# Four edits to the order of work in a two-layer attention and retention trunk: value products, column parts, sine tables, side work

## The chip, the cores and the metric

The kernel runs on one core of one Trainium2 chip. The metric is the device time of one execution in microseconds (us). The kernel before took 2097.04 us, the median of three runs (2094.75, 2097.04 and 2097.13 us).

The core's engines are named as the profile names them: PE (TensorE, the matrix products; PEld is its weight load), DVE (VectorE), ACT (ScalarE), POOL (GpSimd) and SP (SyncE, whose instruction queue starts the DMA transfers).

## What is computed

The input x is 2048 tokens by 1024 channels, in float32. Two layers do x <- x + W_out(concat(A * silu(gA), B * silu(gB))) on h = RMSNorm(x), and a last RMSNorm follows. The reference, cut to the core of one layer:

```python
hn = rms_norm(x, norm_gain)
aq, ak, av, ag, rq, rk, rv, rg = split(hn @ w_in)      # 8 sections of 512 columns
ya = chunked_rel_attention(aq, ak, av, rel_bias)       # 8 heads of 64, band of 9 chunks of 64
yr = chunkwise_retention(rq, rk, rv, cos, sin)         # 4 heads of 128, rotary phases
y  = concatenate([ya * silu(ag), yr * silu(rg)])
x  = x + y @ w_out
```

In the retention, q and k are turned by `cos` and `sin` of position times a frequency, a decayed product inside a chunk is added to a running state, and each head is normalised by its own RMS.

## The kernel before

**Tiles and products.** 2048 tokens are 16 tiles of 128, and four of them make a block n (0 to 3). A float32 matrix product is made of three float16 products of scaled halves (high by high, high by low, low by high), so that a product over 1024 channels is 24 matmuls: 8 channel tiles times 3.

**Stages.** The work of a layer l goes by four head groups s (each two attention heads and one retention head) and, within a group, by the four blocks n. That makes 32 stages (l, s, n). A stage has two halves of dense products:

- `dense_T` (L608 to L735) makes four transposed sections j: q, k, rotary q and rotary k. Each is 24 matmuls of 128x512 (L731) into one bank of the pool `psD`, which has two banks. `evacuate` then copies the bank with ACT (L631, L645) and takes the low half with DVE (`q_rest` L634, `k_rest` L648) one round later; that frees the bank. Sections 2 and 3 go through the rotation (L670, L673, L676), with tables loaded at L616 and L617. The very first stage, (0,0,0), has a form of its own for sections 0 and 1: column parts of 128 tokens (L712), because its tokens come tile by tile.
- `dense_V` (L737 to L772) makes, for each of the four token tiles a, the values of both kinds and both gates: 24 matmuls of 128x512 (L752) into a `psD` bank. ACT copies the value and takes Tanh for the gate (L760, L761, L762, L763), and DVE takes the rests one round later (L766, L768, L770). L770 is the last reader, so that it frees the bank. The gate tile `gt` is from the pool `gp`, with five buffers.

**Rounds.** A half is cut into 12 rounds of 8 matmuls. `run` (L1152) does this for each round: the matmuls of the round; `tick`, which does what was put off by `later(k, fn)`; one step of the attention of the *previous* stage; and some steps of side work, by `pull`. The emission order is the order of PE, DVE, ACT and POOL, each of which works its list strictly in order. SP's order is chosen by a scheduler after the start.

**Attention** goes by 8 units (tile a, head hx), with three rounds each. In the first round of unit i, `flow(1)` takes the value products `pv` of unit i-2 off the list `pipe`, and then `qk` of unit i follows. `qk` has the score matmuls (S, L800 and L801, into the single bank of `psS`), the DVE pass that adds the bias and takes the maximum (`sc`, L804, and `mq`, L806), the exponential (ACT, L807), the split into float16 halves `pq` (ACT L809, POOL L810), and one round later the transposing DMA to `pT` (SP, L812). `sc`, `pq` and `pT` have two buffers each. `pv` multiplies `pT` by the values (L820 to L822: 15 small matmuls for a full band), and `out_` (L826 to L835) divides by the sum, multiplies by the gate and stores, one round later. In the second round the retention's decayed products may follow, in the third the rest of the retention (L860, L864, L868, L880, L908, L916, L920 to L929); the unit's `pv` is then put on `pipe`.

**Side work** is a list of generators with step counts: the norms of the next block's tokens in the first group (`norms_from_input`: L205, L210, L227, L231, and the transposing DMAs L236 and L237 that write the block's `hT`), the rotary tables of the next block (`tables`, L81 to L134, with the two Sin activations at L121 and L122, each block's table being a list of small DVE steps), the scaling and splitting of the next group's weights (waits at L323 are for their mean squares), and `wout_first`, which readies the first two token tiles of the layer's output projection (`y_squares` L958, `y_scale` L961, `rows_hi` L227, `rows_lo` L233, and `y_turn`, again L236 and L237). `wout_first`'s row buffers share their two slots with `sc`. Per round, `run` pulls the number of steps that is the steps left over the rounds left, rounded up:

```python
todo = sum(max(b[1], 0) for b in bg)
...
pull(min(-(-todo // max(left, 1)), todo))
left -= 1
```

After the last group of a layer comes the output projection `wout` (L1105), whose first rounds lie beside the last attention.

Of the kernel before, what the change touches and what calls it, by code (L numbers as in the profile page):

```python
# [10 lines left out]
F32 = mybir.dt.float32  # L11
# [16 lines left out]
def hybrid_trunk(ctx: ExitStack, tc: tile.TileContext, x, pos, gain, gcol, w_in, w_out, rel, fgain,  # L28
# [54 lines left out]
    def tables(n, wk):  # L83

        ang, k, r, k2 = wk
        pi = k2.bitcast(I32)
        for hf in range(2):
            o = n * 512 + hf * 256
            sp.dma_start(pi[hf * 64:(hf + 1) * 64, :], pos[None, o:o + 256].to_broadcast([64, 256]))
        yield  # L90

        def mulsub(dst, kk, c):
            dve.scalar_tensor_tensor(out=dst, in0=kk, scalar=-c, in1=dst, op0=ALU.mult, op1=ALU.add)

        def rnd(dst, src, mul):
            dve.tensor_scalar(dst, src, mul, MAGIC, op0=ALU.mult, op1=ALU.add)
            dve.tensor_scalar(dst, dst, -MAGIC, None, op0=ALU.add)

        dve.tensor_copy(ang, pi)
        dve.tensor_scalar(ang, ang, invf_sb[:, 0:1], None, op0=ALU.mult)  # L100
        yield
        rnd(k, ang, 1.0 / P1)
        yield
        for c in (PA, PB, PC):
            mulsub(ang, k, c)
            yield
        dve.tensor_scalar(k2, k, -(PD + PE_), None, op0=ALU.mult)
        dve.tensor_tensor(k2, k2, ang, op=ALU.add)
        yield
        rnd(k2, k2, 1.0 / TWO_PI)  # L110
        yield
        for kk, c in ((k2, QA), (k, PD), (k2, QB), (k, PE_), (k2, QC)):
            mulsub(ang, kk, c)
            yield
        dve.tensor_scalar(ang, ang, PI_CL, -PI_CL, op0=ALU.min, op1=ALU.max)
        dve.tensor_scalar(k, ang, HALF_PI, -TWO_PI, op0=ALU.is_gt, op1=ALU.mult)
        yield
        dve.tensor_tensor(k, k, ang, op=ALU.add)
        dve.tensor_scalar(k, k, HALF_PI, PI_CL, op0=ALU.add, op1=ALU.min)
        yield  # L120
        act.activation(r, ang, AF.Sin)  # L121
        act.activation(k2, k, AF.Sin)  # L122
        yield
        dve.tensor_scalar(ang, r, -1.0, None, op0=ALU.mult)
        yield
        for hf in range(2):
            sl = slice(hf * 64, hf * 64 + 64)
            cs = slice(hf * 256, hf * 256 + 256)
            sp.dma_start(tab_d[n][0, 0:64, cs], k2[sl, :])
            sp.dma_start(tab_d[n][0, 64:128, cs], k2[sl, :])  # L130
            sp.dma_start(tab_d[n][1, 0:64, cs], ang[sl, :])
            sp.dma_start(tab_d[n][1, 64:128, cs], r[sl, :])
        tab_done.add(n)
        yield  # L134

    TAB_STEPS = 19

    class St:
        pass
# [468 lines left out]
    def dense_T(l, s, n, g, st):  # L608
# [96 lines left out]
        if first:  # L705
# [9 lines left out]
            for j in range(2):  # L715
                evacuate(j, ps[j])
                yield
        for j in range(2 if first else 0, 4):
            if j == 2 and not first:
                tab_load()  # L720
            if first:
                ps = psR.tile([P, 512], F32, tag="small", name=f"dT{nm}_{j}")
            else:
                ps = psD.tile([P, 512], F32, tag="dense", name=f"dT{nm}_{j}")
            while g.tdone <= j:
                pull(1)
            m = 0
            terms = ((g.h, hh), (g.l, hh), (g.h, hl))
            order = [(kt, w) for w in terms for kt in range(KT)] if j == 0 else [(kt, w) for kt in range(KT) for w in terms]
            for kt, (w_, h_) in order:  # L730
                pe.matmul(ps, w_[:, j, kt, :], h_[:, kt, :], start=(m == 0), stop=(m == 23))  # L731
                m += 1
                if m in (8, 16) or (m == 24 and first):
                    yield
            evacuate(j, ps)  # L735
            yield
# [41 lines left out]
    def attention(l, s, n, g, st, prev, nxt):  # L778
        units = []
        for a in range(4):  # L780
            for hx in range(2):
                units.append((a, hx))
        ya = {}

        def qk(a, hx):

            u = St()
            u.a, u.hx = a, hx
            u.nm = f"{l}_{s}_{n}_{a}_{hx}"
            u.nb = nb = min(5, 4 * n + a + 1)  # L790
            u.w = w = nb * P
            u.kts = [(st if t // 4 == n else prev, t % 4) for t in range(4 * n + a + 1 - nb, 4 * n + a + 1)]
            S = psS.tile([P, 1024], F32, tag="S", name=f"S{u.nm}")
            cs = slice(a * P, (a + 1) * P)
            cuts = sorted({0, nb} | {j for j in range(nb) if u.kts[j] == (st, 0) or j == 4})
            for j0, j1 in zip(cuts, cuts[1:]):
                q_, a_ = u.kts[j0]
                k_ = q_.k[:, hx, a_ * P:(a_ + j1 - j0) * P]
                o = S[:, j0 * P:j1 * P]
                pe.matmul(o, st.q[:, hx, 0, cs], k_, start=True, stop=False)  # L800
                pe.matmul(o, st.q[:, hx, 1, cs], k_, start=False, stop=True)  # L801
            v = b2.tile([P, 640], F32, tag="sc", name=f"sc{u.nm}")[:, 0:w]
            m = b2.tile([P, 1], F32, tag="mq", name=f"mq{u.nm}")
            dve.tensor_tensor_reduce(out=v, in0=S[:, 0:w], in1=g.bias[hx][:, 640 - w:640], scale=1.0, scalar=-3.0e38,  # L804
                                     op0=ALU.add, op1=ALU.max, accum_out=m)
            dve.tensor_scalar(m, m, g.nc[:, 0:1], LN_PSC, op0=ALU.mult, op1=ALU.add)  # L806
            act.activation(v, v, AF.Exp, bias=m[:, 0:1], scale=g.c[:, 0:1])  # L807
            pq = b2.tile([P, 1280], F16, tag="pq", name=f"pq{u.nm}")
            act.activation(pq[:, 0:w], v, AF.Copy)  # L809
            pool.tensor_tensor(pq[:, w:2 * w], v, pq[:, 0:w], op=ALU.subtract)  # L810
            u.p = b2.tile([P, 10, P], F16, tag="pT", name=f"pT{u.nm}")[:, 0:2 * nb, :]
            later(1, lambda: sp.dma_start_transpose(out=u.p, in_=pq[:, 0:2 * w]))  # L812
            return u

        def pv(u):
            t = 4 * n + u.a
            o = psR.tile([P, 512], F32, tag="small", name=f"o{u.nm}")
            for b, (q_, a_) in enumerate(u.kts):
                v_ = q_.v[:, a_, u.hx, :]
                pe.matmul(o[:, 0:65], u.p[:, b, :], v_[:, 0:65], start=(b == 0), stop=False)  # L820
                pe.matmul(o[:, 0:64], u.p[:, b, :], v_[:, 65:129], start=False, stop=False)  # L821
                pe.matmul(o[:, 0:65], u.p[:, u.nb + b, :], v_[:, 0:65], start=False, stop=(b == u.nb - 1))  # L822

            def out_():
                rl = b2.tile([P, 1], F32, tag="rl", name=f"rl{u.nm}")
                dve.reciprocal(rl, o[:, 64:65])  # L826
                dve.tensor_tensor(rl, rl, g.ka, op=ALU.mult)
                if u.hx == 0:
                    ya[u.a] = b2.tile([P, P], F32, tag="ya", name=f"ya{u.nm}")
                y = ya[u.a]  # L830
                vs = slice(u.hx * 64, u.hx * 64 + 64)
                dve.scalar_tensor_tensor(out=y[:, vs], in0=o[:, 0:64], scalar=rl[:, 0:1], in1=st.g[u.a][:, vs],
                                         op0=ALU.mult, op1=ALU.mult)
                if u.hx == 1:
                    sp.dma_start(y_d[t][:, s * P:(s + 1) * P], y)  # L835

            later(1, out_)

        ret = retention(l, s, n, g, st)
        for i, (a, hx) in enumerate(units):  # L840
            flow(1)
            u = qk(a, hx)
            yield
            if hx == 1:
                if a < 3:
                    decayed(l, s, n, g, st, a + 1)
                elif nxt is not None:
                    decayed(*nxt, 0)
            yield
            if hx == 1:  # L850
                next(ret, None)
            elif a == 0 and (l, s, n) == (0, 0, 0):
                decayed(l, s, n, g, st, 0)
            pipe.append(lambda u=u: pv(u))
            yield
# [294 lines left out]
        return groups[l, s]  # L1150

    def run(gen, att, thirds):  # L1152
        left = thirds
        for _ in gen:
            tick()
            if att[0] is not None and next(att[0], att) is att:
                att[0] = None
            ring["att_done"] = att[0] is None
            todo = sum(max(b[1], 0) for b in bg)
            if todo == 0 and bg:  # L1160
                todo = 1
            if bg:
                pull(min(-(-todo // max(left, 1)), todo))
            left -= 1

    def norms_from_input(ts, spaces, tab):
# [349 lines left out]
```

## Time and profile before

| quantity | value |
| --- | --- |
| median of three runs | 2097.04 us (2094.75 to 2097.13) |
| the profiled execution, its own time | 2094.75 us |
| its span in the trace | 2092.8 us |
| mean granted PE clock | 0.991 |
| busy: PE, DVE, ACT, POOL | 2004.4, 1343.8, 1141.3, 432.9 us |

The span is what the trace covers of one execution; the execution's own time is 1.95 us longer. In a timeline row the columns are the start in us, the duration in us, engine, line, operation, tiles and shape; what stands in brackets is the idle time of the engine just before, and what ended it. Matmuls overlap one another, so the distance between two starts is what a matmul costs, not its duration. In the view of waits a row gives what the engine waited for, then the total in us, the number of waits and the longest. In the view of windows the columns are the stretch, its length, the busy time and count of PE, PEld, DVE, ACT and POOL, the granted clock, the DMA share and GB/s.

### The profile page before, as it was taken

How to read it: one execution, taken by the hardware profiler on the slowest of the kernel's cores; microseconds unless marked ns; L12 is line 12 of the kernel's file. 1: busy time of each engine (PE TensorE's matmuls, PEld its weight loads, DVE VectorE, ACT ScalarE, POOL GpSimd, SP SyncE). 2: the span in 40 equal slices, each digit the busy share in tenths (PEclk: the TensorE clock that was granted, in tenths of full speed). 3: DMA queues.
4: the chain of work that ended last, by engine and by line, in shares of the span. 5: the costliest groups of instructions: out<-in, count | busy, mean ns of one | idle time of the engine just before them, and what ended most of it. 6: DMA issues, size and time to landing. Idle time of an engine off the chain costs nothing.

```text
span 2092.8 us, 39599 instructions
## 1 busy us (share of the span) xinstructions
PE 2004.4 (96%) x14014; PEld 1049.4 (50%) x14014; DVE 1343.8 (64%) x4031; ACT 1141.3 (55%) x2522; POOL 432.9 (21%) x509
## 2 busy tenths in 40 slices
PE   6888999999999999998999999999999999998998
PEld 4344455555555555444444555555555555554443
DVE  7676666666656666576654666666666667656643
ACT  7455665556565654455444546554655565455432
POOL 1022222222122212121000222222222222222100
PEclk9999999999999999999999999999999999999999
DMA  8767674557476764599965556655655776558874
GB/s 247 171 127 162 136 166 114 115 112 159 110 169 133 161 166 99 113 211 260 219 185 113 120 102 142 130 121 106 155 123 118 178 156 162 117 100 183 212 199 123
DMA packets 645702, 313.65 MB, mean 150 GB/s; under 512 B 459232, under 2 KB 602080, under 8 KB 645504
## 3 DMA queue, kind: packets, MB, share of 16 engines
q1 hardware_dynamic: 645504, 311.12, 66.4%
q8 instruction: 110, 1.80, 0.4%
q14 instruction: 88, 0.72, 0.1%
HBM read 123.26 MB, written 41.98 MB: 79 GB/s over the span
## 4 chain that ended last, share of the span: by engine, by line
PE 55%; DMA 7%; DVE 5%; ACT 3%; issue 1%; SPq 1%; POOL 0%; POOLq 0%; DVEq 0%; ACTq 0%
PE dT L731 18%; PE dV L752 15%; PE dO L1105 12%; DMA pT<-pq 2%; PE r L860 2%; PE S L801 2%; PE S L800 2%; PE o L820 1%; PE o L821 1%; PE o L822 1%; DVE sc L804 1%; DMA swp<-rot 1%; DMA yhy<-rhy 1%; ACT sc L807 1%; ACT pq L809 1%
## 5 line engine op out<-in xcount | busy, mean ns | idle before, releaser
L810 POOL TENSOR_TENSOR pq<-sc,pq 128x640 f16<-128x640 f32 (+4 forms) x256 | 323.8, 1265 | 1175.9 <-issue 590.7
L807 ACT ACTIVATE sc<-sc,mq,cT 128x640 f32<-128x640 f32 (+4 forms) x256 | 218.5, 853 | 558.1 <-DVE mq L806 413.7
L752 PE MATMUL dV<-whV,hTh 128*128 128x512 f16 x1024 | 354.5, 382 | 13.0 <-DVE gt L770 12.8
L731 PE MATMUL dT<-hTh,whT 128*128 128x512 f16 x1008 | 349.4, 382 | 14.7 <-DMA hTh<-hTl 9.6
L752 PE MATMUL dV<-wlV,hTh 128*128 128x512 f16 x1024 | 354.1, 381 | 0.0
L752 PE MATMUL dV<-whV,hTl 128*128 128x512 f16 x1024 | 354.0, 381 | 0.0
L731 PE MATMUL dT<-hTl,whT 128*128 128x512 f16 x1008 | 346.6, 379 | 0.0
L731 PE MATMUL dT<-hTh,wlT 128*128 128x512 f16 x1008 | 346.6, 379 | 0.0
L752 PEld LDWEIGHTS <-hTh 128*128 128x128 f16 x2048 | 197.3, 98 | 227.7 <-DVE gt L770 16.4
L731 PEld LDWEIGHTS <-whT 128*128 128x128 f16 x2016 | 192.9, 98 | 221.6 <-issue 24.1
L804 DVE CUSTOM_DVE_ANT_0 sc<-S,bias 128x640 f32<-128x640 f32 (+4 forms) x256 | 188.4, 736 | 78.8 <-PE S L801 61.1
L1105 PE MATMUL dO<-whO,yly 128*128 128x512 f16 x512 | 194.1, 379 | 2.4 <-DMA yly<-rly 2.4
L1105 PE MATMUL dO<-whO,yhy 128*128 128x512 f16 x512 | 194.0, 379 | 1.2 <-DVE gt L770 0.6
L1105 PE MATMUL dO<-wlO,yhy 128*128 128x512 f16 x512 | 194.0, 379 | 0.0
L809 ACT ACTIVATE pq<-sc 128x640 f16<-128x640 f32 (+4 forms) x256 | 171.5, 670 | 10.9 <-DMA pT<-pq 3.0
L1105 PEld LDWEIGHTS <-yhy 128*128 128x128 f16 x1024 | 99.6, 98 | 115.1 <-issue 0.8
L752 PEld LDWEIGHTS <-hTl 128*128 128x128 f16 x1024 | 99.7, 98 | 105.0 <-issue 2.8
L800 PE MATMUL S<-k,q 128*128 128x128 f16 (+3 forms) x592 | 143.1, 268 | 7.9 <-DVE mq L804 7.9
L731 PEld LDWEIGHTS <-wlT 128*128 128x128 f16 x1008 | 97.2, 98 | 101.8 <-issue 1.1
L820 PE MATMUL o<-v,pT 128*128 128x65 f16 x1120 | 129.6, 193 | 10.2 <-DMA pT<-pq 9.7
L801 PE MATMUL S<-k,q 128*128 128x128 f16 (+3 forms) x592 | 130.5, 268 | 0.0
L820 PEld LDWEIGHTS <-pT 128*128 128x128 f16 x1120 | 105.3, 97 | 49.2 <-DMA pT<-pq 21.3
(350 smaller groups left out, 3352.7 us busy)
## 6 DMA issues: line engine op xcount, KB each, us to landing
q<-qq SPq DMA_DIRECT2D x128, 128.0 KB, 2.7
yyy<-y_d SPq DMA_DIRECT2D x32, 512.0 KB, 4.6
stT<-in_w_in_dram SPq DMA_DIRECT2D x27, 512.0 KB, 4.8
stV<-in_w_in_dram SPq DMA_DIRECT2D x26, 512.0 KB, 4.5
k<-kk SPq DMA_DIRECT2D x128, 64.0 KB, 2.0
swp<-rot SPq DMA_DIRECT2D x64, 128.0 KB, 2.5
tabc<-tab SPq DMA_DIRECT2D x32, 256.0 KB, 2.7
tabs<-tab SPq DMA_DIRECT2D x32, 256.0 KB, 2.9
```

What stands on the lines that cost most here:

```text
L731: pe.matmul(ps, w_[:, j, kt, :], h_[:, kt, :], start=(m == 0), stop=(m == 23))
L752: pe.matmul(ps, h_[:, kt, a * P:(a + 1) * P], w_[:, kt, :], start=(m == 0), stop=(m == 23))
L800: pe.matmul(o, st.q[:, hx, 0, cs], k_, start=True, stop=False)
L801: pe.matmul(o, st.q[:, hx, 1, cs], k_, start=False, stop=True)
L804: dve.tensor_tensor_reduce(out=v, in0=S[:, 0:w], in1=g.bias[hx][:, 640 - w:640], scale=1.0, scalar=-3.0e38, op0=ALU.add, op1=ALU.max, accu ...
L807: act.activation(v, v, AF.Exp, bias=m[:, 0:1], scale=g.c[:, 0:1])
L809: act.activation(pq[:, 0:w], v, AF.Copy)
L810: pool.tensor_tensor(pq[:, w:2 * w], v, pq[:, 0:w], op=ALU.subtract)
L820: pe.matmul(o[:, 0:65], u.p[:, b, :], v_[:, 0:65], start=(b == 0), stop=False)
L821: pe.matmul(o[:, 0:64], u.p[:, b, :], v_[:, 65:129], start=False, stop=False)
L860: pe.matmul(out_, w_, m_, start=(i == 0), stop=(i + 1 == len(pairs)))
L1105: pe.matmul(ps, h_[:, kt, :], w_[:, kt, :], start=(m == 0), stop=(m == 23))
```

## The change

Four edits are made together.

1. `tables` gets one more empty step ahead of the two Sin activations, for every block but 0, and its count of steps goes from 19 to 20.
2. `dense_T` does sections 0 and 1 of stages (0,0,1), (0,0,2) and (0,0,3) in eight column parts of 128 tokens: three parts of q, three of k, the last of q, the last of k. A part is 24 matmuls of 128x128; there are 32 of them to a round, and six rounds as before. Both sections are evacuated in the sixth round.
3. In the attention, `qk` of unit i comes ahead of the value products, and these come one round later, in the unit's second round, ahead of `decayed`.
4. `run` pulls side steps by a running sum of steps left over rounds left, from a debt of one half, instead of rounding up in every round.

```diff
@@ tables
         dve.tensor_scalar(k, k, HALF_PI, PI_CL, op0=ALU.add, op1=ALU.min)
         yield
+        if n:
+            yield
         act.activation(r, ang, AF.Sin)
         act.activation(k2, k, AF.Sin)
-    TAB_STEPS = 19
+    TAB_STEPS = 20
@@ dense_T
-        for j in range(2 if first else 0, 4):
+        parts = (l, s) == (0, 0) and n > 0
+        if parts:
+            ps, m = [None] * 2, 0
+            for (j, a) in ((0, 0), (0, 1), (0, 2), (1, 0), (1, 1), (1, 2), (0, 3), (1, 3)):
+                if a == 0:
+                    ps[j] = psD.tile([P, 512], F32, tag="dense", name=f"dT{nm}_{j}")
+                cs = slice(a * P, (a + 1) * P)
+                for i in range(24):
+                    w_, h_ = ((g.h, hh), (g.l, hh), (g.h, hl))[i // KT]
+                    pe.matmul(ps[j][:, cs], w_[:, j, i % KT, :], h_[:, i % KT, cs], start=(i == 0), stop=(i == 23))
+                    m += 1
+                    if m % 32 == 0 and m < 192:
+                        yield
+                if a == 3:
+                    evacuate(j, ps[j])
+            yield
+        for j in range(2 if first or parts else 0, 4):
@@ attention
         for i, (a, hx) in enumerate(units):
+            u = qk(a, hx)
+            yield
             flow(1)
-            u = qk(a, hx)
-            yield
             if hx == 1:
@@ run
-        left = thirds
+        left, debt = thirds, 0.5
...
             if bg:
-                pull(min(-(-todo // max(left, 1)), todo))
+                debt += todo / max(left, 1)
+                pull(min(int(debt + 0.01), todo))
+                debt -= int(debt + 0.01)
             left -= 1
```

More of the change, by code (lines that the diff above doesn't have):

```diff
@@ L840, in attention @@
         for i, (a, hx) in enumerate(units):
-            flow(1)
             u = qk(a, hx)
             yield
+            flow(1)
             if hx == 1:
```

## The prediction

> **What bounds the kernel now.** I read the busy line of the page first, then the view of PE's waits, then windows of the places where those waits are, then timelines there.
>
> ```profile
> PE 2004.4 (96%) x14014; PEld 1049.4 (50%) x14014; DVE 1343.8 (64%) x4031; ACT 1141.3 (55%) x2522; POOL 432.9 (21%) x509
> PE dV L752 <- DVE gt L770: 12.8, 6, 4.9
> PE o L820 <- DMA pT<-pq: 9.7, 11, 2.2
> PE dT L731 <- DMA hTh<-hTl: 9.6, 1, 9.6
> PE S L800 <- DVE mq L804: 7.9, 4, 3.3
> PE msT L323 <- DVE mbT L316: 3.3, 3, 1.9
> PE msV L323 <- DVE ya L832: 2.9, 2, 1.6
> PE dT L731 <- DMA hTh<-rhn: 2.8, 1, 2.8
> ```
>
> PE is busy for 2004.4 of the span's 2092.8 us, so only some 88 us of idle time can be taken away, and the change adds no speed to a matmul. These seven rows of waits hold 49 us. The windows say where they lie (PE's busy time is the second number):
>
> ```profile
> 104.00:141.00 37.00, 27.64 (x162) 13.03 (x161) 27.33 (x77) 22.82 (x53) 7.67 (x11) 0.95 0.68 130
> 166.00:205.00 39.00, 29.46 (x209) 15.60 (x207) 27.29 (x74) 23.23 (x49) 7.98 (x10) 0.91 0.81 177
> 340.00:620.00 280.00, 278.64 (x2060) 148.31 (x2059) 185.31 (x605) 163.22 (x384) 66.09 (x74) 1.00 0.60 127
> 860.00:900.00 40.00, 33.77 (x239) 17.40 (x238) 25.22 (x76) 22.94 (x48) 6.74 (x7) 0.91 0.76 156
> 1870.00:1910.00 40.00, 33.56 (x251) 17.87 (x250) 25.25 (x72) 23.04 (x47) 7.16 (x8) 0.96 0.67 143
> ```
>
> From 340 to 620 us PE idles for 1.4 us: the steady stages have nothing to give. The idle time is in the first head group (9.4 us in 104 to 141, 9.5 in 166 to 205) and at the last stage of each layer (6.2 and 6.4 us of 40). The granted clock is below 1 in just these windows; a timeline shows what that is.
>
> ```profile
> 129.54 0.61 PE L752 MATMUL dV<-whV,hTh 128*128 128x512 f16 x1 [4.88 <-DVE gt L770]
> 129.94 0.63 PE L752 MATMUL dV<-whV,hTl 128*128 128x512 f16 x1
> 130.37 0.63 PE L752 MATMUL dV<-wlV,hTh 128*128 128x512 f16 x1
> 132.93 0.20 PE L820 MATMUL o<-v,pT 128*128 128x65 f16 x1
> 133.20 0.38 PE L800 MATMUL S<-k,q 128*128 128x512 f16 x1
> 133.63 0.38 PE L752 MATMUL dV<-wlV,hTh 128*128 128x512 f16 x1
> 133.85 0.38 PE L752 MATMUL dV<-whV,hTh 128*128 128x512 f16 x1
> ```
>
> After 4.88 us of idleness the matmuls start 0.43 us apart, and from 133 on 0.215 us (0.22 by these rounded rows). So such a wait costs its idle time and then about 0.2 us for each of the next 8 matmuls, 1.7 us here. The busy time hides that second part.
>
> **Sine tables a round later, and even side steps (first group, n = 1 and 2).** The wait above is for a bank. Its tile's matmuls were long over, and ACT stood before the Sin work:
>
> ```profile
> 115.95 0.38 PE L752 MATMUL dV<-wlV,hTh 128*128 128x512 f16 x1
> 124.36 1.28 ACT L121 ACT_TABLE_LOAD   x1
> 126.28 0.26 ACT L760 ACTIVATE v<-dV 128x128 f16<-128x128 f32 x1
> 126.54 1.28 ACT L761 ACT_TABLE_LOAD   x1
> ```
>
> PE ended tile a=1 at 116.2. ACT came to it at 126.28, after norms and then 1.92 us of Sin with its table, and lost 1.28 more going back to Tanh: 3.2 us. In the changed order Sin comes after a=1's evacuation and ahead of a=2's, whose bank is wanted three rounds later. The wait of 4.88 falls by 3.2, and at 1.7 us PE would not slow: 3.2 + 1.7 = 4.9. I take **+5** for n=1 (gains are positive); bounds -2 (Sin is as much in the way of a=2, and the even spread leaves more norm steps in the second half of the stage) and +8 (most of the 9.4, plus slow matmuls). For n=2 the window has the same idle time, but the norms' chain is as full: **+2.5**, bounds 0 to +6.
>
> **Column parts (first group).** The start of (0,0,1) and of (0,0,3):
>
> ```profile
> 69.37 1.29 SPq L237 DMA_TRANSPOSE hTl<-hTl  x1
> 74.73 2.92 SPq L237 DMA_TRANSPOSE hTl<-hTl  x1
> 78.11 0.69 DVE L670 TENSOR_TENSOR raw<-raw,tabc 128x512 f32<-128x512 f32 x1 [7.20 <-DMA swp<-raw]
> 78.91 3.26 PE L731 MATMUL dT<-hTh,whT 128*128 128x512 f16 x8 [9.64 <-DMA hTh<-hTl]
> 81.10 0.41 DVE L770 SCALAR_TENSOR_TENSOR gt<-gt,dV 128x256 f32<-128x256 f32 x1
> 204.90 3.40 PE L731 MATMUL dT<-hTh,whT 128*128 128x512 f16 x8 [2.81 <-DMA hTh<-rhn]
> ```
>
> PE waits 9.64 us for the last token tile's transposed copy, issued at 74.73; the three tiles before were issued by 70.7 (69.37 + 1.29). With parts, three q parts can run from about 73. But the three k parts need the second bank, and that is freed by L770 at 81.10, which stands in DVE's order behind the wait that ends at 78.11; this order is unchanged. So five parts are left at 81.5: 5 x 24 x 56 ns (below) = 6.7, to 88.2, and some 2 us more for a slow start after the new idle time. In the kernel before, 8 matmuls are done at 82.1 and 40 x 0.215 = 8.6 lead to 90.7. The gain of about 0.5 goes into section 2: both banks are evacuated in one round, and it has to wait for ACT and DVE. I take **-1**, bounds -4 and +2. At (0,0,3) the bank is free, the three early parts hide the wait of 2.81, and the 8 matmuls in 3.24 us (to 208.14, with 1.72 at full rate) go faster: 2.8 + 1.5 = 4.3, of which I take **+3** (0 to +4.3). The wait for the banks at section 2 costs (0,0,2) and (0,0,3) about 1 us each, an ACT copy and a DVE rest less 24 short matmuls: **-2** (-4 to 0).
>
> What the parts cost in themselves:
>
> ```profile
> 33.89 0.61 PE L712 MATMUL dT<-hTh,wlT 128*128 128x128 f16 x8
> 34.33 0.61 PE L712 MATMUL dT<-hTh,whT 128*128 128x128 f16 x8
> L820 PEld LDWEIGHTS <-pT x1120: 95/96/152, 93.4 to 1967.8; 128*128 128x128 f16 x187
> ```
>
> The first stage has such parts: eight in 0.44 to 0.45 us, 56 ns each. A section is 96 of them, 5.38 us, against 24 x 0.2155 = 5.17. Six sections: **-1.3**, bounds -26 (rival 4) and 0. The Trainium skill, "TensorE: Matmul & The Clock Gate", section "Back-to-back issue gap", gives about 81 ns a matmul for N=128 and 131 ns for N=512 in a stream of weight loads and matmuls; by it, estimated, a section would go from 3.1 to 7.8 us and the six would cost 28 us. The rows above, 56 and 215 ns, do not agree with it.
>
> **Even side steps elsewhere.** Group (0,0)'s last stage waits for mean squares (msT 3.3, msV 2.9 in all): fewer weight steps in its early rounds, **+2** (-2 to +5). The larger case is the last stage of each layer:
>
> ```profile
> 877.29 0.82 DVE L804 CUSTOM_DVE_ANT_0 sc<-S,bias 128x640 f32<-128x640 f32 x1 [5.11 <-DMA yhy<-rhy]
> 878.17 0.27 PE L800 MATMUL S<-k,q 128*128 128x128 f16 x1 [3.28 <-DVE mq L804]
> 879.19 0.63 PE L752 MATMUL dV<-wlV,hTh 128*128 128x512 f16 x1
> 883.87 0.38 PE L752 MATMUL dV<-whV,hTl 128*128 128x512 f16 x1
> 1891.00 0.27 PE L800 MATMUL S<-k,q 128*128 128x128 f16 x1 [3.18 <-DVE mq L804]
> ```
>
> The score buffer `sc` shares its slots with the row buffers of `wout_first`, so DVE's pass waits 5.11 us for the DMA that reads a row, and PE waits 3.28 for the score bank. Then 11 matmuls go 0.43 us apart (879.19 to 883.87), 2.3 us lost: 5.6 here, and the same at 1891.00 (3.18 and, the clock of that window being higher, some 1.4). Nineteen side steps are left for 12 rounds there: rounded up that is two a round, spread evenly 1.6. The second token tile's row then takes its slot only after this unit's `sc`. I take **+9.5** for both layers; bounds 0 (another unit meets the row instead) and +12.7 (the two windows' 12.6 us of idle time). What is late next is ACT's square of that tile, which nothing on PE needs at once.
>
> **Value products a round later.** The eleven waits for `pT` come to 9.7 us, the longest 2.2, the mean 0.9. A round has 8 x 0.2155 = 1.72 us of dense matmuls and the attention's besides, so one round covers all but the longest: **+8**, bounds 0 and +10. `qk` first means that PE no longer has the products ahead of S, nine in 0.27 us (132.93 to 133.20; fifteen, 0.45), while it waits for the score bank: **-1** over the run (-3 to 0). A wait is added on SP: `pT` has two buffers, so unit i+2's transposing DMA now waits for products of unit i in the same round, with the stores of L835 and L927 and other loads behind it in the queue. It costs nothing while `pq` is later still:
>
> ```profile
> L810 POOL TENSOR_TENSOR pq<-sc,pq 128x640 f16<-128x640 f32 (+4 forms) x256 | 323.8, 1265 | 1175.9 <-issue 590.7
> ```
>
> L804 (0.82) and L810 (1.27) alone are 2.1 us, over the 1.72 of a round, and the exponential and its copy come on top.
>
> **Sum.** 5 + 2.5 - 1 + 3 - 2 - 1.3 + 2 + 9.5 + 8 - 1 = 24.7 us. The profiled execution took 2094.75 us, with a span of 2092.8: it becomes 2070. The median is 2.3 higher, so the forecast is **2072**.
>
> **Rivals.**
>
> 1. *The first group gives nothing*: DVE, with 27.3 us in a window in which PE has 27.6, or a bank is late in the same way. The 7.5 us of its gains and losses go, or turn to -5: 24.7 - 7.5 - 5 = 12, 2080 to 2085. For it speaks the bank at 81.10.
> 2. *The `pT` waits move with the products*, as the DMAs come later by the added wait on SP: 2072 + 8 = 2080. Against it, the L810 row.
> 3. *Slower.* The fifth gate buffer: Tanh (L761) of tile a=3 needs the buffer that `out_` of unit 5 reads, and that is now emitted in the very round that ends a=3. If DVE is over a round (1.7 us) behind PE there, ACT stands, the bank comes late, and the next stage's second section waits. One us in each of 31 stages is 31: 2072 + 31 = 2103. It decides once ACT's delay is over the three rounds until that bank is wanted. ACT is usually early here, so I give it little:
>
> ```profile
> ACT v L760 <- PE dV L752: 22.4, 22, 3.4
> ```
>
> 4. *Weight loads bound the parts*: at the 96 ns of the LDWEIGHTS row a section takes 9.2 us, 4.05 more, 24 in all: 2072 + 23 = 2095. The skill's rule points here; the 56 ns speak against it.
> 5. *The score slot is met all the same* at the layer's end, by another unit: 2072 + 9.5 = 2081.
>
> **Numbers.** Forecast 0.56, rival 1 0.15, rival 2 0.09, rival 3 0.08, rival 4 0.04, rival 5 0.08. A measurement of this kernel tells about 0.2%, 4.2 us, from no change. Faster: 0.56 + 0.15 + 0.09 + 0.08, less a little for rivals that come together, 0.86; within 0.2%: rival 4 and that little, 0.06; slower 0.08. The range takes in rivals 1, 2 and 5 and two of them together (2092), and below it the upper bounds of the large terms: n=1 +3, layer ends +3, `pT` +2, n=2 +3.5, which give 2060. Rivals 3 and 4 are left out.
>
> **What would show it.** Right: the rows PE o <- pT and PE S <- mq nearly gone; no PE wait over 1 us in the last stage of either layer; the 4.88 row shrunk or gone; idle time at about 82 us, not before 73, in (0,0,1). Parts at 56 ns apart. Wrong: waits of ACT's L761 (then L779) for DVE in many stages, PE waits for L770 in the steady window, or side work that is late for the output projection (L1105 waiting for y's rows).

## The result, and the profile after

The changed kernel took 2124.95 us (median of four runs, 2122.47 to 2127.13), and the kernel before 2097.09 us beside it. The ratio is 1.0134, with a 95% interval of 1.0117 to 1.0152. It is 28 us slower where 25 us less were forecast, and outside the range given. The profiled execution has a span of 2124.8 us, against 2092.8 before.

In all that follows line numbers are those of the kernel at hand: from `dense_V` on the changed kernel's are 18 higher, so that L752, L770, L804, L832 and L860 before are L770, L788, L822, L850 and L878 after.

PE's busy line and waits in the changed kernel (columns of the waits: total in us, number, longest):

```profile
PE 2018.8 (95%) x14446; PEld 1075.7 (51%) x14446; DVE 1334.5 (63%) x4031; ACT 1142.9 (54%) x2522; POOL 431.1 (20%) x509
PE r L878 <- DVE ya L850: 19.7, 10, 2.7
PE dT L729 <- DVE gt L788: 12.8, 5, 6.3
PE S L818 <- DVE mq L822: 10.7, 8, 2.5
PE dV L770 <- DVE gt L788: 7.0, 4, 3.4
PE dT L749 <- DVE qq L636: 4.6, 3, 2.0
PE msT L325 <- DVE ya L850: 3.9, 9, 0.7
PE o L838 <- DMA pT<-pq: 2.3, 1, 2.3
```

Most of the waits at which the forecast aimed are down: `pT` from 9.7 us to 2.3, the dense bank in `dense_V` from 12.8 to 7.0, the transposed copies (9.6 and 2.8) gone. The score bank (`S`) is not: 10.7 us in 8 waits, against 7.9 in 4; the two long ones at the layer ends are down to one of 2.00 us (at 901.49), and others have come elsewhere (2.25 us at 112.55, 2.45 at 636.68, 2.24 at 1664.99). Three rows stand there that the kernel before did not have: retention products (`r`) and mean squares (`msT`) that wait for `out_` (tile `ya`), and the column parts (L729) that wait for the second dense bank.

The same windows as before, by time from the start:

```profile
104.00:141.00 37.00, 28.62 (x185) 14.16 (x184) 26.58 (x74) 19.96 (x44) 6.31 (x8) 0.91 0.49 103
166.00:205.00 39.00, 34.78 (x283) 19.22 (x281) 30.83 (x83) 23.55 (x51) 10.13 (x12) 1.00 0.75 152
340.00:620.00 280.00, 275.05 (x2015) 146.23 (x2013) 181.59 (x602) 157.42 (x370) 65.65 (x74) 1.00 0.57 121
860.00:900.00 40.00, 39.49 (x306) 21.43 (x305) 24.41 (x72) 20.49 (x42) 8.29 (x9) 1.00 0.64 120
1870.00:1910.00 40.00, 40.00 (x307) 21.63 (x306) 23.81 (x68) 17.42 (x39) 10.11 (x10) 1.00 0.54 101
```

From 340 to 620 us PE is now idle for 4.95 us where it was 1.4. Windows by time shift against each other (the last two now lie ahead of the waits at the layer ends), so the place of a loss is better read from the work. Each kernel has the same dense work, 7680 matmuls of 512 columns (a part of 128 columns counts a quarter). The table compares the start of the same one in two traces, in us after the kernel before (differences in the text are taken before rounding); a layer's 16 stages are 192 each, and its output projection is 768.

| run | end of the first group (768) | start of layer 0's last stage (2880) | start of its projection (3072) | start of layer 1 (3840) | start of layer 1's last stage (6720) | start of its projection (6912) | last |
| --- | --- | --- | --- | --- | --- | --- | --- |
| changed kernel | +4.3 | +18.9 | +14.5 | +19.2 | +34.3 | +27.7 | +32.3 |
| without edit 3 | +7.6 | +19.1 | +13.0 | +14.4 | +24.3 | +18.8 | +20.6 |
| edit 4 alone | +12.1 | +26.2 | +20.5 | +25.1 | +34.1 | +28.9 | +30.6 |
| 4, at the layer ends only | -0.7 | -0.3 | -6.2 | -4.8 | -4.3 | -10.1 | -7.4 |
| 4, in the first group only | +12.6 | +12.8 | +12.6 | +13.6 | +14.4 | +14.5 | +13.9 |
| 4, in the steady stages only | -0.6 | +9.2 | +9.1 | +8.3 | +17.6 | +18.2 | +18.2 |
| edit 3 alone | -4.3 | -1.9 | -0.7 | +0.4 | +1.4 | +4.5 | +4.3 |
| 3, with `out_` at once | -4.4 | -6.2 | -6.3 | -5.8 | -8.6 | -7.9 | -8.0 |

The changed kernel gains 4.4 and 6.6 us at the two layer ends, near the 9.5 forecast for both, and loses 4 us in the first group, 15 us in the steady stages of each layer, and 5 us in each projection. The forecast had counted the steady stages (all but the first group and the layer ends) at nothing but a gain.

### The profile page after: what moved, and what is told of

Its sections match the earlier page's. It is cut to its first block, busy times and chain, and to the rows that moved or that the text cites. A ratio compares the mean times of both kernels' runs of the same rounds, so it can differ in the third digit from the quotient of the medians.

```text
span 2124.8 us, 40468 instructions
## 1 busy us (share of the span) xinstructions
PE 2018.8 (95%) x14446; PEld 1075.7 (51%) x14446; DVE 1334.5 (63%) x4031; ACT 1142.9 (54%) x2522; POOL 431.1 (20%) x509
## 5 line engine op out<-in xcount | busy, mean ns | idle before, releaser
L770 PE MATMUL dV<-whV,hTh 128*128 128x512 f16 x1024 | 359.1, 387 | 7.8 <-DVE gt L788 7.0
L770 PE MATMUL dV<-whV,hTl 128*128 128x512 f16 x1024 | 353.9, 381 | 0.0
L770 PE MATMUL dV<-wlV,hTh 128*128 128x512 f16 x1024 | 353.2, 381 | 0.0
L749 PE MATMUL dT<-hTh,whT 128*128 128x512 f16 x960 | 331.8, 379 | 4.6 <-DVE qq L636 4.6
L749 PE MATMUL dT<-hTh,wlT 128*128 128x512 f16 x960 | 331.8, 379 | 0.0
L749 PE MATMUL dT<-hTl,whT 128*128 128x512 f16 x960 | 331.8, 379 | 0.0
L770 PEld LDWEIGHTS <-hTh 128*128 128x128 f16 x2048 | 196.1, 99 | 211.7 <-issue 10.1
L749 PEld LDWEIGHTS <-whT 128*128 128x128 f16 x1920 | 181.6, 98 | 180.8 <-issue 0.7
L822 DVE CUSTOM_DVE_ANT_0 sc<-S,bias 128x640 f32<-128x640 f32 (+4 forms) x256 | 187.8, 734 | 36.6 <-PE S L819 30.2
L818 PE MATMUL S<-k,q 128*128 128x128 f16 (+3 forms) x592 | 144.1, 269 | 11.6 <-DVE mq L822 10.7
L770 PEld LDWEIGHTS <-hTl 128*128 128x128 f16 x1024 | 99.9, 98 | 101.3 <-issue 2.9
L749 PEld LDWEIGHTS <-wlT 128*128 128x128 f16 x960 | 92.5, 98 | 98.8 <-issue 6.1
L886 DVE SCALAR_TENSOR_TENSOR sh<-sh,state 128x128 f16<-128x128 f16 x120 | 93.7, 781 | 74.0 <-ACT sh L882 74.0
```

The source lines that it names most:

```text
L770: pe.matmul(ps, h_[:, kt, a * P:(a + 1) * P], w_[:, kt, :], start=(m == 0), stop=(m == 23))
L886: dve.scalar_tensor_tensor(out=dst[:, 1], in0=dst[:, 0], scalar=-2.0 ** 11, in1=src, op0=ALU.mult, op1=ALU.add)
```

## The experiments

Twelve kernels, each against runs of the kernel before on the same chip. First the edits one by one.

**e1, the changed kernel without edit 3.**

```diff
-            u = qk(a, hx)
-            yield
-            flow(1)
+            flow(1)
+            u = qk(a, hx)
+            yield
```

> The changed kernel with the value products back in the unit's first round ahead of the scores (edits 1, 2 and 4 stay). Theory A (the bank): the loss of 28 us comes from the retention and mean-square products, which wait for the small PSUM bank that the value products' out_ frees one round later. Undone, the 19.7 us of waits 'PE r <- DVE ya' and the 3.9 of 'msT <- DVE ya' go, with the slow matmuls behind them, some 8 us of pT waits come back, and the layer ends keep their gain of 11: about 2088 to 2096. Theory B (column parts and first group): the loss is made before 300 us and stays, 2120 or more (with the pT waits back, up to 2133).

Measured: 2116.79 us against 2095.96, ratio 1.0092 (1.0077 to 1.0108). Neither theory: edit 3 makes only some 8 us of the 28, and the loss is not all made in the first group either (7.6 of the 20.6 us that this trace is behind at its last matmul). The waits for `ya` are gone, but those for `pT` come back at more than the 8 us expected:

```profile
PE o L838 <- DMA pT<-pq: 19.8, 15, 5.1
```

**e2, edit 3 alone** (the same lines the other way round, on the kernel before).

> Only edit 3 on the kernel before: qk first, value products a round later. Theory A: 20 to 25 us of new waits for the small banks less 8 of pT waits, and no gain at the layer ends: 2109 to 2122. Theory B: only the pT waits change, about 2089.

Measured: 2099.99 against 2095.96, ratio 1.0017 (1.0008 to 1.0026). The new waits a little more than eat the gain; theory A has the mechanism and not the size. The row of the score bank has grown too, from 7.9 us. The waits in this run:

```profile
PE S L800 <- DVE mq L804: 13.5, 9, 5.5
PE r L860 <- DVE ya L832: 4.7, 4, 2.8
PE msT L323 <- DVE ya L832: 4.6, 6, 1.7
PE o L820 <- DMA pT<-pq: 3.3, 3, 2.3
```

**e3, edit 2 alone**: the block that begins with `parts = ...`, on the kernel before.

> Only edit 2 on the kernel before: sections 0 and 1 of the three stages in column parts. In the changed kernel PE waits there for the second dense bank (6.3, 3.3 and 2.8 us) and for the evacuation ahead of section 2 (1.1, 2.2, 1.8), against 9.6 + 2.8 us of waits for the transposed copies before. Theory A: the parts cost little, 2093 to 2104. Theory B: they make the whole loss, 2120 or more.

Measured: 2096.30 against 2095.96, ratio 1.0002 (0.9991 to 1.0012): no difference. The wait for the last token tile is replaced by the wait for the second bank, as in the changed kernel, where the timelines of PE and DVE read:

```profile
73.07 0.61 PE L729 MATMUL dT<-hTl,whT 128*128 128x128 f16 x8
79.96 1.03 PE L729 MATMUL dT<-hTh,whT 128*128 128x128 f16 x8 [6.28 <-DVE gt L788]
80.78 1.06 PE L729 MATMUL dT<-hTh,wlT 128*128 128x128 f16 x8
```

```profile
76.50 0.69 DVE L672 TENSOR_TENSOR raw<-raw,tabc 128x512 f32<-128x512 f32 x1 [6.74 <-DMA swp<-raw]
79.49 0.41 DVE L788 SCALAR_TENSOR_TENSOR gt<-gt,dV 128x256 f32<-128x256 f32 x1
```

The three q parts run to about 73.5, and then PE sits idle until DVE, held at L672 by a DMA up to 76.50, has done L788. After 6.28 us of idleness eight matmuls of a part take some 0.84 us (79.96 to 80.78 to 81.64) and not 0.45.

**e4, edit 4 alone.**

```diff
-                pull(min(-(-todo // max(left, 1)), todo))
+                debt += todo / max(left, 1)
+                pull(min(int(debt + 0.01), todo))
+                debt -= int(debt + 0.01)
```

> Only edit 4 on the kernel before: even side steps. The step of the prediction on the layer ends says 9.5 us there, and the trace of the changed kernel shows 4.4 and 6.6 us less up to the output projection; the first group may move by 5 either way. If that gain is of this edit alone: 2081 to 2092. If it needs the other edits: 2095 or more.

Measured: 2126.41 against 2095.96, ratio 1.0139 (1.0123 to 1.0155). Wrong in sign: this edit alone loses as much as all four together. The gain of the expectation is there, in its place: from the start to the end of each last stage the traces have -5.7 and -5.1. From here on the question was where edit 4 loses, so it was done in one place at a time, with a switch to `run` and the same three lines behind it:

```diff
-    def run(gen, att, thirds):
+    def run(gen, att, thirds, even=False):
...
-                run(dense_V(l, s, n, g, st), att, 24 if n == NS - 1 and s < NSW - 1 else 12)
+                run(dense_V(l, s, n, g, st), att, 24 if n == NS - 1 and s < NSW - 1 else 12, s == NSW - 1 and n == NS - 1)
```

**e5, at the layer ends only.**

> On the kernel before, even side steps only in the value half of the last stage of each layer. Theory C (place): edit 4 gains where rounding up pulled two steps a round, at the two layer ends (5.7 and 5.1 us in the run with edit 4 alone), and loses everywhere else. Then this is about 11 faster, 2083 to 2088. Theory D: the even steps hand the work of the layer end to the output projection, which was 4.6 and 1.7 us slower in that run: 2089 to 2093.

Measured: 2086.65 against 2094.94, ratio 0.9964 (0.9952 to 0.9977). Both theories are in it: 5.8 and 5.7 us are gained up to the projection, and about 2 us of each are given back in the projection's first stretch (by the traces +2.2 from matmul 3072 to 3264 and +2.2 from 6912 to 7104). PE's waits for the score bank, 7.9 us in 4 before with the longest 3.3, are now

```profile
PE S L800 <- DVE mq L804: 2.0, 4, 0.8
```

**e6, in the first group only** (`even` is `(l, s) == (0, 0)`, in both halves).

> On the kernel before, even side steps only in the stages of the first head group. Theory C: the last token tile's norm comes at the end of the stage, its transposing DMAs are issued two rounds later, and the next stage, which has no column parts here, waits for them (14.1 and 12.3 us in the run with edit 4 alone, against 2.8 and 2.2): the 12 us that run had lost after the first group, so 2105 to 2112. If the loss is not made there: 2098 or less.

Measured: 2108.82 against 2094.94, ratio 1.0067 (1.0054 to 1.0080). Theory C. SP's timeline has the last tile's copies of block 2 in the kernel before:

```profile
136.18 1.57 SPq L236 DMA_TRANSPOSE hTh<-rhn  x1
139.23 1.33 SPq L237 DMA_TRANSPOSE hTl<-rln  x1
```

and in this run, with PE's first row of stage (0,0,2) and its largest waits:

```profile
145.71 1.41 SPq L236 DMA_TRANSPOSE hTh<-rhn  x1
147.16 1.31 SPq L237 DMA_TRANSPOSE hTl<-rln  x1
```

```profile
149.32 3.57 PE L731 MATMUL dT<-hTh,whT 128*128 128x512 f16 x8 [13.32 <-DMA hTh<-rhn]
```

```profile
PE dT L731 <- DMA hTh<-rhn: 13.3, 1, 13.3
PE dT L731 <- issue: 12.2, 1, 12.2
```

The copies are issued 8 to 9.5 us later and PE waits 13.3 us. The row of 12.2 us is the start of (0,0,3), where the view names no releaser. In the changed kernel, where the column parts begin with the other three token tiles, both rows are gone. The first group costs 4.3 us there, 7.6 without edit 3 (e1), and 12.1 with edit 4 alone; edit 3 alone takes 4.3 off, so the parts are not all of that difference.

**e7, in the steady stages only** (`even` is `(l, s) != (0, 0)`, without the value half of the layer ends).

> On the kernel before, even side steps in all stages but those of the first group and the value half at the layer ends. Theory C: one or two us in each stage in which weights are split, 14 in layer 0 and 9 in layer 1 by the run with edit 4 alone: 2114 to 2122. If those stages only carried on a disturbance of the first group: 2094 to 2102.

Measured: 2114.99 against 2094.94, ratio 1.0093 (1.0078 to 1.0108). Theory C: 9.8 us in layer 0 and 9.3 in layer 1, from stages that PE had filled. Counted stage by stage as in the table, the loss is not spread over all of them: six stages, the first (n = 0) of each head group after a layer's first, lose 1.5 to 3.0 us each, the stages (0,2,2) and (1,2,2) lose 2.4 and 2.8, and no other steady stage more than 0.3. One such place, at the end of the transposed half of stage (0,2,0), in which the value weights' last steps are done. DVE in the kernel before:

```profile
493.36 0.16 DVE L407 TENSOR_TENSOR gqkV<-gqkV 128x1 f32<-128x1 f32 x1 [2.89 <-ACT reV L404]
495.35 1.29 DVE L333 SCALAR_TENSOR_TENSOR wlV<-stV,sV,whV 128x1024 f16<-128x1024 f32 x1 [0.22 <-ACT whV L330]
496.55 0.28 DVE L868 SCALAR_TENSOR_TENSOR sh<-sh,state 128x128 f16<-128x128 f16 x1
```

and DVE and PE in e7:

```profile
498.11 0.16 DVE L407 TENSOR_TENSOR gqkV<-gqkV 128x1 f32<-128x1 f32 x1 [5.39 <-ACT reV L404]
500.11 1.28 DVE L333 SCALAR_TENSOR_TENSOR wlV<-stV,sV,whV 128x1024 f16<-128x1024 f32 x1 [1.00 <-ACT whV L330]
501.31 0.29 DVE L868 SCALAR_TENSOR_TENSOR sh<-sh,state 128x128 f16<-128x128 f16 x1
```

```profile
499.91 0.27 PE L860 MATMUL r<-sh,rot 128*128 128x128 f16 x2
501.65 0.22 PE L860 MATMUL r<-sh,rot 128*128 128x128 f16 x1 [1.47 <-DVE sh L868]
```

The weight scale's chain of small instructions goes to and fro between ACT and DVE, and DVE stands still for it, 2.89 us before and 5.39 now. By PE's count of matmuls it is 1.25 rounds later, with passes over the weights behind it, in the rounds in which DVE must give the retention its halves (L868). PE stands at the third product of the retention until DVE gets there. The same wait of `r` for `sh`, of 1.46 to 2.22 us, stands at the same point of all six first stages; before, it stood at none of them. In (0,2,2) and (1,2,2) PE waits for the score bank, 2.61 and 2.81 us.

**e9, the same, a step sooner.**

```diff
-        left, debt = thirds, 0.5
+        left, debt = thirds, 0.98
```

> As the run with even steps in the steady stages, but the running sum starts at 0.98 in place of 0.5, so that a step comes about half a round sooner, and hardly ever later than in the kernel before. Theory F (lateness): those stages lose because the weight scaling is one round later all the way and its last steps meet the retention and the value products; then most of the 20 us goes, 2094 to 2101. Theory G (spreading): steps at even distance are worse in themselves than steps at the front: 2108 or more.

Measured: 2094.89 against 2092.96, ratio 1.0009 (0.9999 to 1.0018). Theory F: the 20 us are gone. In most of these stages about one step is left per round, so rounding up and the running sum do nearly the same things, and with 0.98 the order is almost that of before. What e7 changed was mainly the start of the sum, which puts the steps about a round back. Spreading as such was thereby hardly tried.

Then edit 3 again, now with the bank freed sooner.

**e8, edit 3 with `out_` at once.**

```diff
-            later(1, out_)
+            out_()
```

> Edit 3 on the kernel before, and out_ emitted right behind the value products instead of a round later, so that it stands ahead of the next round's side work on DVE. Theory A: the retention and mean-square products then no longer wait for the bank that out_ reads (4.7 and 4.6 us of 'r <- ya' and 'msT <- ya' with edit 3 alone), and the 6 to 8 us of pT waits that edit 3 takes away show: 2084 to 2092. Rival E: DVE itself now waits for the products, and delays scores and rests: 2100 or more.

Measured: 2088.46 against 2094.94, ratio 0.9964 (0.9952 to 0.9977). Theory A, in the middle of its range. In this trace no row of `r` or `msT` waiting for `ya` is left, and `pT` has one wait:

```profile
PE dV L752 <- DVE gt L770: 12.6, 6, 4.6
PE S L800 <- DVE mq L804: 10.3, 6, 4.4
PE o L820 <- DMA pT<-pq: 2.8, 1, 2.8
```

**e10, e8 and e5 together.**

> Even steps at the layer ends only, value products a round later, out_ at once. The two gains of 8.3 and 6.5 us lie in different places and should add: 2078 to 2083. If the layer end's wait for the score slot and the moved products share one cover: 2085 or more.

Measured: 2081.03 against 2092.96, ratio 0.9937 (0.9924 to 0.9951). They add up to 11.9 us of the 14.8 that the two have alone, within what can be told. This version beats both kernels.

**e11, e10 with the column parts.**

> The same with the column parts of edit 2. Alone they gave nothing: 2.2 us gained by the end of the first group and lost again later. If the later loss was of the pT waits and banks that this version no longer has: 2074 to 2079. If the parts only trade the wait for the last token tile against the wait for the second bank: 2080 to 2084.

Measured: 2081.34 against 2092.96, ratio 0.9938 (0.9926 to 0.9951): no gain over e10. Its second row of waits is `dT L727 <- DVE gt L786`, 8.2 us in 3, so the parts again trade one wait for the other.

**e12, edit 1 alone** (the empty step ahead of Sin, and `TAB_STEPS` 20).

> Only edit 1 on the kernel before: Sin a round later. By the step of the prediction the bank wait of 4.9 us in (0,0,1) falls by 3.2 and the slow matmuls behind it by 1.7: with the second table some 5 to 9 us, 2087 to 2092. If Sin meets the next evacuation in the same way: 2095 to 2100.

Measured: 2097.36 against 2092.96, ratio 1.0017 (1.0008 to 1.0026). By the medians a little slower, by the profiled execution the same (a span of 2092.1 against 2092.8). The wait at which it aimed did fall, from 4.88 us to 1.44, and the next one grew, from 2.21 to 4.79:

```profile
126.44 0.39 PE L754 MATMUL dV<-whV,hTh 128*128 128x512 f16 x1 [1.44 <-DVE gt L772]
138.02 2.21 PE L733 MATMUL dT<-hTh,whT 128*128 128x512 f16 x5 [4.79 <-DVE r L882]
```

## Why the prediction was wrong, step by step

- **What bounds the kernel.** The reading of the waits was right: each row that it named could be made smaller, and most were. But "the steady stages have nothing to give" was read as if they had nothing to lose. A stretch in which PE idles for 1.4 us of 280 can hold results of DVE and ACT that come just in time, and edit 4 puts the weight steps ahead of them about a round back. This is the step that failed: edit 4's cost there was put at nothing, and no reason was given. It measured 20 us (e7), in eight stages, with 14 more in the first group (e6), which the forecast had only in a lower bound of -2, and 8 gained at the layer ends (e5); these make some 25 of the 30 of e4. Of the rest, 2.4 us lie in stage (0,3,0): PE waits there 2.38 us for `pT` in e4 (at 739.80) and then runs at half rate for 3.4 us, while in e7 it waits 1.64 us and runs on at full rate. Some 3 lie in the first projection.
- **Sine tables, +5 and +2.5.** The mechanism and even the size were right at its place: 4.88 less 3.2 was to leave 1.7 us and no slow matmuls, and e12 has 1.44 and full rate. But the end of that stage is set by the next block's tokens: the wait at the start of (0,0,2) went from 2.21 to 4.79 us. A lead of 4.8 us behind the bank wait is down to 1 us a few matmuls into the next stage, and e12 as a whole shows none.
- **Column parts, -1 and +3 and -2 and -1.3.** The bank of the second section was seen for (0,0,1): idle from about 73 to about 81 was worked out, and 6.28 us were measured, to 79.96. It was not seen for the other two stages, where PE also waits for L788 (3.15 us at 147.83, 2.61 at 211.72). For the parts in themselves the 56 ns held: eight in 0.45 us in the warm rows (72.62 to 73.07), so that the 81 ns of the Trainium skill, "TensorE: Matmul & The Clock Gate", section "Back-to-back issue gap", is not met here either, and rival 4 falls. (Its bound of -26 counted the 1.3 twice: six times 4.05 is 24.) Summed, -1.3 was forecast for the parts and 0 measured (e3), within what can be told.
- **Even side steps elsewhere, +2 and +9.5.** The +2 for mean squares in group (0,0)'s last stage is borne out in e6: the wait of `msT` for its squares is 0.8 us against 3.3, and the stage is 3.6 us shorter, though it starts 16.2 us late. The layer ends are right in mechanism and a little high in size: 11.6 us up to the projections, 7.5 to 8 at the end (e5). The first stretch of the projection gives the rest back; its products wait for `dense_V`'s last banks (L770, 3.6 us in 4, against 0.6) and for the output weights' low halves (1.5 us).
- **Value products, +8 and -1.** `pT` gave 7.4 us, as forecast. The -1 for the score bank was too small: its waits grew by 5.6 us in e2 and by 2.4 in e8. What was missed is the bank of `o`. It comes from a pool of four small banks that the retention products and the mean squares share, and it is free when `out_` has read it. One row of the prediction's own list, `msV` waiting 2.9 us for `ya`, was a wait of this kind. With the products one round later, `out_` stands in DVE's list behind the weight passes of that round, and the next user of the bank is due on PE at once:

```profile
508.17 1.28 DVE L335 SCALAR_TENSOR_TENSOR wlV<-stV,sV,whV 128x1024 f16<-128x1024 f32 x1 [1.01 <-ACT whV L332]
510.15 0.28 DVE L850 SCALAR_TENSOR_TENSOR ya<-o,rl,gt 128x64 f32<-128x64 f32 x1
```

```profile
510.58 0.27 PE L878 MATMUL r<-rv,dT 128*128 128x128 f16 x2 [2.33 <-DVE ya L850]
```

  That took 9.3 us alone (e2) and 23.6 with the other edits; six of the ten waits of `r` in the changed kernel stand at the same point as e7's, the end of the transposed half in the first stage of a later group, so that the two losses meet there. e8 shows that it was this and not the wait added on SP: with `out_` at once the forecast +7 is there (6.5 measured). Rival 3 looked at the same late `out_`, at another buffer. ACT's Tanh does wait for it more than before,

```profile
ACT gt L761 <- DVE ya L832: 0.5, 1, 0.5
ACT gt L779 <- DVE ya L850: 5.0, 4, 1.9
```

  but in four places (the first row is of before) and not in 31 stages; two of them, at 146.13 and 210.02, are just ahead of PE's waits for the second bank of the column parts.
- **The sum.** Every gain of the sum was about a wait that could be seen. What decided was work that could not be seen as a wait in the steady window, since its cover was complete. The rival that would have won was "the steps of edit 4 come one round later, meet the retention where a head group begins, and cost 1.5 to 3 us in each of eight stages; in the first group they make the next block's tokens late", which the prediction did not have. (Two of the rivals it had can reach 2095 together, 2085 and 9.5, not 2092.)

## What to carry to other kernels

When a rule that orders side work is changed, price it in the stages that are full, not only in those with idle time: ask for each step what it is in time for, and by how many rounds. When a product is moved later, follow its output bank to whoever gets that bank next, and move the reader that frees it along with the product, ahead of the side work. Make such edits one at a time and in one place: here the useful place of edit 4 lay under its losses in the first group and in eight steady stages, and edit 3 paid only once `out_` was moved along; the two together are worth 12 us (e10).

## What was not expected of the hardware

That matmuls run at about half rate after 4.88 us of idleness was in the prediction. It holds for parts of 128 columns as for 512 (0.84 us for eight against 0.45, and 0.43 us against 0.215 for one). Not expected was that stretches at half clock also follow waits of 2.0 to 2.8 us. Of two like waits in the changed kernel, 2.33 us up to 510.58 (shown above) and 2.35 us here, the first is followed by a granted clock of 1.00, the second of 0.59:

```profile
724.06 0.27 PE L878 MATMUL r<-rv,dT 128*128 128x128 f16 x2 [2.35 <-DVE ya L850]
511.00:514.40 3.40, 3.40 (x24) 1.85 (x22) 3.35 (x7) 2.35 (x4) 0.68 (x1) 1.00 0.71 186
724.50:728.40 3.90, 3.90 (x18) 1.88 (x16) 3.83 (x8) 2.34 (x4) 1.21 (x1) 0.59 0.70 190
```

So in these traces the length of a wait alone does not tell whether the clock falls; what else decides is not shown. By the clock's records in the trace it is at a half in five stretches of the changed kernel's steady stages (from 298.5, 636.5, 725.2, 1329.4 and 1752.6 us, the first of 6.8 us, the others of 3.4), and in none of those of the kernel before. Estimated at half of their length they cost some 10 us, a third of what the steady stages lose, on top of the waits ahead of them. A wait of 5 us costs some 7 by the row at 129.54, and e12's cut from 4.88 to 1.44 was worth more at its place than the cut itself: 5.1 us.

What stays open: the other 2 us that layer 0's steady stages lose with edit 4 everywhere and not in e7, and why the projections lose 5 us each in the changed kernel, where they lose 1.4 and 1.8 without edit 3 (e1). In part that is a stretch of 3.4 us at half clock in each (from 984.6 and 1943.8 us), which e1 has in neither; estimated as above, 1.7 us. Even spreading of the side steps without the shift by a round was not tried.
